# A decoder layer on one core: SBUF from the dynamic-transfer reserve, used for the last block's attention, ysT, five of FF1's joins and W1's pieces

## The chip, the core and the metric

The kernel runs on one core of one Trainium2 chip. The metric is device time in microseconds (us) of one execution, lower is better. Times before are the median of three runs; the profile is of one more execution. PE is TensorE, DVE is VectorE, ACT is ScalarE, POOL is GpSimd, SP is SyncE, which here issues nearly all transfers between HBM and SBUF.

## What is computed

One layer on x of 2048 rows by 1024 columns, in float32:

```python
a = rms_norm(h, pre_mix_g)
q, k, v, f, u_sg, v_sg = split(a @ w_in)
y_att = forgetting_attention(q, k, v, f + f_bias)        # 8 heads x 64, causal
y_sg = chunked_spatial_gating(u_sg, v_sg, ...)           # chunks of 128 rows
y = concat([rms_norm(y_att, att_out_g), rms_norm(y_sg, sg_out_g)])
h = h + rms_norm(y @ w_out, post_mix_g)
c = rms_norm(h, pre_ffn_g)
ff = square(relu(c @ w_ff1)) @ w_ff2                     # 1024 -> 4096 -> 1024
h = h + rms_norm(ff, post_ffn_g)
h = h + sigmoid(h @ ple_gate_w + ple_gate_b) * (p @ ple_w)
```

## The kernel before

**Precision.** Each large product is made of three matmuls (`mm3`, lines 102 to 106): operands are split into a higher half, a copy rounded to float32r, and a lower half, the rest. ACT mostly makes the higher halves and DVE the lower ones (`halves_of`, `evac_split`).

**Order.** The program is written in one order of emission, with fillers (`Filler`, `Spread`) that draw some steps of a side job per step of the main one. A planner then fixes each engine's list and the places of all tiles: it takes, for every engine, the earliest emitted instruction that its model of the time holds to be ready. So an instruction may stand far ahead of its place in the code, but on the chip each engine works through its list in order, and a wait holds up all that is behind it. SP's list of transfers is such a list too. A tile that is allotted where closed tiles were has to wait for the last use of those.

**Stages.** First the input projection, gating, and the maxima of the scores; then attention over four blocks of 512 rows, with the output projection of finished blocks (`project`, lines 695 to 810) drawn in between; then FF1, FF2 and the gate. FF1 and FF2 use a scheme with seven products in place of eight over 2x2 block matrices, so FF1's right operands B[m][k] (m = 1 to 7, k = 0 to 3) are sums and differences of pieces of the normed, turned h ("joins").

**Around the end of attention.** `finish(k)` (lines 676 to 693) takes a head's result, transposes it, divides it and stores it through `yo` to attS in HBM. `project(b)` goes over four tiles of 128 rows: it loads the attention rows `yn` (line 700), squares and norms them (706, 710), transposes them (766), splits them into `yaT` (769), and multiplies them and `ysT`, the gating's rows (714), with w_out, 16 steps of three matmuls for each tile, numbered `n`; the step at which the next tile is squared is `YSQ` (8), the one at which it is normed `YNO` (13). `ysT` has one place; its next load is emitted at its last use, step 11 of a tile. Results go through `z`, are normed and added to x, and are stored to hS (742 to 757). For the last block only the first row tile's last head goes into `yn` directly; the other three tiles come back from HBM.

With the last block's projection (`last_proj`, line 1122) runs `prep_first` (lines 1083 to 1095) as a filler, 16 parts over 54 steps: it loads pieces of hS into `px` tiles (three places) and `v_t`, `x_t`, scales them (POOL, 1013), transposes them (PE, 1018) and makes B for k = 0 and 1 on the spot (`join_now`), and stores the pieces of k = 2 and 3 to cS in HBM (1028). After the loop, `join_load` brings k = 2 back (1033), and `join(2)` starts with its three plain pieces. Then the pools of the projection and of w_out (`wide`) are closed. Only then are `w1p`, the three places of W1's split pieces, allotted (line 1134), as are the remaining B of k = 2 and 3 (`ctb`) and the joins' results j and inputs r (`jt`). The rest of join 2 and all of join 3 are emitted between the first seven products of FF1 (`join_rest`, `JR`).

FF1 (`run`, `left`, `ff1`) has 32 units; a unit has seven products of 4 x 3 matmuls. The first unit goes twice over its seven products, for k = 0, 1 first and k = 2, 3 after. `left` (1157 to 1181) makes W1's sums in `ws` on DVE (1170) and splits them into `w1p` (991 on ACT, 994 on DVE). The second half of the rows gets its B from `prep_next` (1097 to 1107), whose two held pieces lie in `px` too.

Of the kernel before, what the change touches and what calls it, by code (L numbers as in the profile page):

```python
# [9 lines left out]
F32 = mybir.dt.float32  # L10
# [24 lines left out]
def trunk(ctx, tc, x, p, w_in, f_bias, sg_ln_g, sg_ln_b, sg_w, sg_b, att_out_g, sg_out_g,  # L35
# [640 lines left out]
    def finish(k):  # L676

        b, h = heads[k]
        os = osp.tile([HD + 1, TB], F32, name="os")
        sc.copy(os, outs.pop(k)[:HD + 1])  # L680
        yield
        yt = pT.tile([P, 4, P], F32, name="pT")
        for tt in range(4):
            pe.transpose(yt[:, tt, :HD + 1], os[:, tt * P:(tt + 1) * P], ident[:HD + 1, :HD + 1])
        l = small.tile([P, 4], F32, name="l")
        ve.reciprocal(l, yt[:, :, HD])
        yo = small.tile([P, 4, HD], F32, name="yo")
        if k == len(heads) - 1:

            ve.tensor_tensor(tail_yn[0][:, AW - HD:], yt[:, 0, :HD], l[:, 0:1].broadcast_to([P, HD]), ALU.mult)  # L690
        ve.tensor_tensor(yo, yt[:, :, :HD], l.unsqueeze(2).broadcast_to([P, 4, HD]), ALU.mult)
        sy.dma_start(attS[b * TB:(b + 1) * TB, h * HD:(h + 1) * HD].rearrange("(a p) d -> p a d", p=P), yo)
        yield

    def project(b):

        def load(tt, width=AW):
            r0 = b * TB + tt * P
            yn = yp.tile([P, AW], F32, name="yn", bufs=2)
            sy.dma_start(yn[:, :width], attS[r0:r0 + P, :width])  # L700
            return yn
# [10 lines left out]
        def load_ys(tt):  # L712
            t = yp.tile([P, 4, 2, P], F32R, name="ysT")
            sy.dma_start(t.bitcast(F32), ysS[4 * b + tt])
            return t

        last = b == NB - 1
        ys_t = load_ys(0)
        yn = load(0, AW - HD if last else AW)
        if last:  # L720
            tail_yn.append(yn)
        yield
# [39 lines left out]
        for tt in range(4):  # L762
# [4 lines left out]
            if tt < 3:  # L767
                yn = load(tt + 1)
            ya_t = yp.tile([P, 2, 4, P], F32R, name="yaT", bufs=2)
# [10 lines left out]
            for hf, kcs in parts:  # L780
                if kcs[0] == 4:
                    nm = "pM" if pm_free and nb % 3 else "pW"
                    pss.append((pM if nm == "pM" else pW).tile([P, 512], F32, name=nm))
                    nb += 1
                for kc in kcs:
                    mm3(pss[hf], yT[kc], (w_o[kc][hf][:, 0], w_o[kc][hf][:, 1]), kc == 4, kc == 1)
                    if rest:
                        rest.popleft()()
                    if n in (6, 7):
                        xs.append(yp.tile([P, 512], F32, name="xt2", bufs=2))  # L790
                        sy.dma_start(xs[-1], x[r0:r0 + P, (n - 6) * 512:(n - 5) * 512])
                    if tt < 3:
                        if n == YSQ:
                            r_yn = square(yn)
                        if n == YNO:
                            normal(yn, r_yn)
                        if hf == 1 and kc == 7:
                            ys_t = load_ys(tt + 1)
                    if kc == 1:
                        zs[hf] = yp.tile([P, 512], F32, name="z2", bufs=2)  # L800
                        sc.copy(zs[hf], pss[hf])
                        junk = yp.tile([P, AW], F32, name="yjunk")
                        sc.activation(junk, zs[hf], AF.Square, accum_out=ss2[:, hf:hf + 1])
                    n += 1
                    yield
            tail(r0, zs, xs, ss2)
        while rest:
            rest.popleft()()
            if not last:
                yield  # L810

    YSQ, YNO = 8, 13
    MASKB = 4
    PREPT = 54
# [148 lines left out]
    ws = [fsm.tile([P, 4, P], F32, name=f"ws{e}") for e in range(2)]  # L963
    px = [w1q.tile([P, 4, P], F32, name=f"px{e}") for e in range(3)]

# [7 lines left out]

    _, w1raw = w1_places(w1q)

    LATE = (6, 3, 7, 2, 4)
    B = [[None] * KH for _ in range(8)]
    early = [ctx3.tile([P, 2, 512], F32R, name=f"B{m}_2") for m in (1, 3, 2)]  # L980
    kept = [ctx3.tile([P, 2, 512], F32R, name=f"B{m}_1") for m in LATE]
    for k in range(2):
        for m in range(1, 8):
            B[m][k] = kept[LATE.index(m)] if k and m in LATE else cta.tile([P, 2, 512], F32R, name=f"B{m}_{k}")
    for m, t in zip((1, 3, 2), early):
        B[m][2] = t
# [48 lines left out]
    def join(k, place, raws):  # L1035

        ra, rd, rc, rb = raws
        halves_of(B[1][k], ra, "pool", "dve")
        yield
        halves_of(B[3][k], rd, "act", "dve")  # L1040
        yield
        halves_of(B[2][k], rc, "act", "dve")
        yield
        t1, t2, t3, t4 = (place() for _ in range(4))
        for m, t, x, y, e in ((5, t1, rb, ra, po), (6, t2, rd, t1, ve), (7, t3, rd, rb, po), (4, t4, t2, rc, ve)):
            e.tensor_tensor(t, x, y, ALU.subtract)
            halves_of(B[m][k], t, "act", "dve")
            yield
# [31 lines left out]

    flat = [t.rearrange("p a b -> p (a b)") for t in px]

# [14 lines left out]
    def prep_next():  # L1097

        for k in (3, 2, 1, 0):
# [6 lines left out]

            yield from join_now(k, 1, place, done, flat[0], flat[1], px[2], px[2])

    raws, nraw, nleft = {}, 2, 0
    lefts = {}  # L1110
# [9 lines left out]
    load_w1(0, 0)  # L1120
    pfill = Filler(prep_first(), 16, PREPT)
    for n, _ in enumerate(last_proj):
        pfill.tick()
    pfill.drain()
    jraw = [flat[e] for e in range(3)] + [w1raw[1].rearrange("p k f -> p (k f)")[:, :512]]
    join_load(2, jraw)
    pl = []
    join2 = join(2, lambda: pl.pop(0), jraw)
    for _ in range(3):
        next(join2)  # L1130
    ph.close()
    pmph.close()
    mix_stack.close()
    w1p = w1_pieces(pool(w1s, "w1pp", side="right"))

# [104 lines left out]

    pl += [jt.tile([P, 512], F32, name=f"j{e}") for e in range(6)] * 2
    jraw3 = [jt.tile([P, 512], F32, name=f"r{e}") for e in range(4)]
    join_load(3, jraw3)

    def join_rest():
        join3 = join(3, lambda: pl.pop(0), jraw3)
        for _ in range(3):
            next(join3)
            yield
        for _ in range(4):  # L1250
            next(join2)
            yield
            next(join3)
            yield
# [103 lines left out]
    hold = first_of[NF + 2]  # L1358
    JR = (1, 1, 2, 2, 2, 2, 1)

    NEXT = [[(1, 2), (1, 3)], [(5, 2), (5, 3)], [(6, 1)], [(3, 1), (6, 2), (6, 3)], [(7, 1), (3, 2), (3, 3)],
            [(2, 1), (7, 2), (7, 3)], [(4, 1), (2, 2), (2, 3), (4, 2), (4, 3)]]
    for i, (u, n, ks) in enumerate(run):
        if i == len(JR):
# [3 lines left out]
            ctc = pool(fl, "ctc")  # L1368
            hqp = pool(fl, "hqp")
            for t in ((0, 0), (0, 1), (1, 0), (1, 1), 5, 6):  # L1370
                hq[t] = hqp.tile([P, 512], F32, name="hq" + str(t).strip("()").replace(", ", "_"))
# [50 lines left out]
    RR += [w1all.rearrange("p a k f -> p (a k f)")[:, e * 512:(e + 1) * 512] for e in range(4)]  # L1422
    wple = early + [kept[3]]
    wple = [wple[:2], wple[2:]]
# [197 lines left out]
```

## Time and profile before

| | |
|---|---|
| median of three runs | 2703.38 us (2702.57 to 2706.26) |
| profiled execution | 2701.87 us |
| its span | 2700.1 us |
| TensorE clock granted, mean | 0.989 |
| PE idle, 1123.7 to 1190.5 us (last block's projection) | 9.75 us of 66.80 |
| PE idle, 1190.5 to 1204.0 us (before FF1) | 13.5 us of 13.5 |
| DVE busy, 1190.5 to 1204.0 us | 13.06 us |

All times in the profile are microseconds from the start of the span. A row of the line of time has its start, its length, the engine, the line of the code (that of a helper, where one records the operation), the operation, out<-in, shapes and count; in brackets stands how long the engine was idle before it and what released it. A wait for several things is put down to the one that came last.

### The profile page before, as it was taken

The numbers are of one execution on the slowest core, as the hardware profiler recorded it, in microseconds if no ns is written. First come the engines' busy times: TensorE is split into PE (matmuls) and PEld (weight loads), VectorE is DVE, ScalarE is ACT, GpSimd is POOL, SyncE is SP. The second block draws the span as 40 slices with busy tenths as digits, with TensorE's granted clock in tenths as the row PEclk, the third lists the DMA queues.
The fourth block names the chain that finished last, engine by engine and source line by source line (L and its number), as shares of the span: only waits on it lengthen the run. The fifth ranks groups of instructions, "written<-read, shape, count | busy, mean of one in ns | idle before, by whom it ended". The sixth has DMA issues, their size and how long they took to land.

```text
span 2700.1 us, 37436 instructions
## 1 busy us (share of the span) xinstructions
PE 2613.7 (97%) x12316; PEld 2123.4 (79%) x12316; DVE 1841.5 (68%) x3212; ACT 1342.4 (50%) x2632; POOL 811.5 (30%) x695
## 2 busy tenths in 40 slices
PE   8999999999899999969999999999999999999999
PEld 7787978777677777757788788888888888888887
DVE  5547576866778655578888676668886596875443
ACT  6444433358777777555555554544445444453111
POOL 5444343510000000253444332325451171501211
PEclk9999999999999999989999999999999999999999
DMA  5565756598868766454665854447556654673331
GB/s 169 151 183 145 195 141 171 145 218 211 210 177 190 175 182 151 137 164 165 224 210 175 296 193 148 150 155 247 171 191 223 187 160 132 210 250 115 109 119 61
DMA packets 440611, 472.85 MB, mean 175 GB/s; under 512 B 155616, under 2 KB 269664, under 8 KB 440416
## 3 DMA queue, kind: packets, MB, share of 16 engines
q1 hardware_dynamic: 430179, 454.39, 57.0%
q10 hardware_dynamic: 10237, 16.07, 2.2%
q8 instruction: 97, 1.59, 0.3%
q14 instruction: 98, 0.80, 0.1%
HBM read 336.38 MB, written 133.96 MB: 174 GB/s over the span
## 4 chain that ended last, share of the span: by engine, by line
PE 53%; DMA 2%; DVE 1%; issue 1%; ACT 1%; POOL 0%; SPq 0%; DVEq 0%; ACTq 0%; POOLq 0%
PE pf L106 17%; PE pf L104 17%; PE pf L105 17%; PE pf L1470 1%; DMA w1raw<-in_w_ff_dram 0%; DMA px<-hS 0%; DMA cS<-px 0%; DVE w1p L994 0%; DMA B<-jS 0%; PE pf L1018 0%; DVE ws L1170 0%; DVE hq L1189 0%; DVE z L748 0%; POOL tmp L1068 0%; DMA ysT<-ysS 0%
## 5 line engine op out<-in xcount | busy, mean ns | idle before, releaser
L104 PE MATMUL pf<-B,w1p 128*128 128x512 f32 x752 | 298.3, 397 | 14.4 <-ACT w1p L991 13.6
L106 PE MATMUL pf<-B,w1p 128*128 128x512 f32 x752 | 296.1, 394 | 2.8 <-DVE w1p L994 2.7
L1197 POOL TENSOR_TENSOR hq<-hq,hq 128x512 f32<-128x512 f32 x128 | 197.0, 1550 | 335.4 <-ACT hq L1191 298.3
L105 PE MATMUL pf<-B,w1p 128*128 128x512 f32 x752 | 297.1, 395 | 0.0
L660 DVE TENSOR_TENSOR hl<-pr,hl 128x512 fp32r<-128x512 f32 (+1 forms) x320 | 191.9, 608 | 102.7 <-ACT hl L659 86.0
L100 POOL TENSOR_TENSOR wsp<-wraw,wsp 128x344 fp32r<-128x344 f32 (+1 forms) x176 | 200.1, 1154 | 192.0 <-ACT wsp L96 181.6
L651 ACT ACTIVATE pr<-pS,bias 128x512 f32<-128x512 f32 (+1 forms) x320 | 196.6, 623 | 106.1 <-PE pS L647 64.0
L172 DVE TENSOR_REDUCE mx<-pM 128x1 f32<-128x512 f32 (+3 forms) x288 | 169.8, 597 | 78.7 <-PE pM L169 78.0
L104 PEld LDWEIGHTS pf<-B,w1p 128*128 128x128 f32 x752 | 141.7, 188 | 48.9 <-ACT w1p L991 14.1
L104 PE MATMUL pacc<-wsp,wide 128*128 128x344 f32 (+1 forms) x480 | 166.7, 347 | 9.7 <-ACT ug L358 6.8
L104 PE MATMUL pf<-R,L 128*128 128x512 f32 x452 | 175.9, 389 | 0.0
L106 PE MATMUL pf<-R,L 128*128 128x512 f32 x452 | 175.8, 389 | 0.0
L105 PE MATMUL pf<-R,L 128*128 128x512 f32 x452 | 175.8, 389 | 0.0
L106 PEld LDWEIGHTS pf<-B,w1p 128*128 128x128 f32 x752 | 141.5, 188 | 37.5 <-DVE w1p L994 4.4
L105 PEld LDWEIGHTS pf<-B,w1p 128*128 128x128 f32 x752 | 141.7, 188 | 31.9
L106 PE MATMUL pacc<-wsp,wide 128*128 128x344 f32 (+1 forms) x480 | 162.7, 339 | 0.5 <-DVE wide L117 0.5
L105 PE MATMUL pacc<-wsp,wide 128*128 128x344 f32 (+1 forms) x480 | 162.4, 338 | 0.0
L659 ACT CAST hl<-pr 128x512 fp32r<-128x512 f32 (+3 forms) x272 | 146.6, 549 | 6.5 <-PE pO L674 0.8
L991 ACT CAST L<-lr 128x512 fp32r<-128x512 f32 x113 | 70.3, 622 | 149.6 <-PE pf L105 119.5
L994 DVE TENSOR_TENSOR L<-lr,L 128x512 fp32r<-128x512 f32 x113 | 96.1, 851 | 68.0 <-ACT L L991 67.7
L994 DVE TENSOR_TENSOR w1p<-ws,w1p 128x512 fp32r<-128x512 f32 (+1 forms) x136 | 117.4, 869 | 35.7 <-ACT w1p L991 33.8
L991 ACT CAST w1p<-w1raw 128x512 fp32r<-128x512 f32 (+1 forms) x123 | 73.4, 598 | 128.5 <-PE pf L105 124.2
(443 smaller groups left out, 7199.1 us busy)
## 6 DMA issues: line engine op xcount, KB each, us to landing
hidC<-hq SPq DMA_DIRECT2D x224, 256.0 KB
lr<-hidC SPq DMA_DIRECT2D x224, 256.0 KB
w1raw<-in_w_ff_dram SPq DMA_DIRECT2D x64, 512.0 KB
w1raw<-in_w_ff_dram SPq DMA_DIRECT2D x128, 256.0 KB
wraw<-in_w_in_dram SPq DMA_DIRECT2D x96, 256.0 KB
wraw<-in_w_in_dram SPq DMA_DIRECT2D x88, 172.0 KB
KM<-kS ACTq DMA_DIRECT2D x80, 132.0 KB
jS<-C SPq DMA_DIRECT2D x19, 512.0 KB
```

Of the source, the lines that this page charges most:

```text
L100: e.tensor_tensor(dst[:, 1], src, dst[:, 0].bitcast(F32), ALU.subtract)
L104: pe.matmul(ps, l[0], r[0], start=first, stop=False)
L105: pe.matmul(ps, l[0], r[1], start=False, stop=False)
L106: pe.matmul(ps, l[1], r[0], start=False, stop=last)
L172: ve.tensor_reduce(mx[:, tt, c:c + 1], ps[:, :full], AX.X, ALU.max)
L651: sc.activation(pr[:, off:], ps[:, off:], AF.Exp, bias=bias_of(b)[:, j, h:h + 1])
L659: sc.copy(hl[:, 0, off:], pr[:, off:])
L660: ve.tensor_tensor(hl[:, 1, off:], pr[:, off:], hl[:, 0, off:].bitcast(F32), ALU.subtract)
L991: sc.copy(dst[:, 0], src)
L994: (po if lo == "pool" else ve).tensor_tensor(dst[:, 1], src, dst[:, 0].bitcast(F32), ALU.subtract)
L1197: po.tensor_tensor(t, x, y, op)
L1470: pe.transpose(ps[:, kk], hts[t][g][:, kk * P:(kk + 1) * P], ident)
```

## The change

The kernel is built with 1 KB for each partition reserved for dynamic transfers in place of 16. In the places gained:

- The four `yn` tiles of the last block are loaded when its projection begins, without the last head's 64 columns; `finish` of the last head writes these into all four, and its store to attS goes. `yn` has four places, two before. For this block the next tile is squared at step 2 and normed at step 7.
- `ysT` has two places; a tile's `ysT` is loaded at the start of the tile before.
- Two of the three `px` tiles are the `ws` tiles; `prep_next` has two tiles of its own for its held pieces (`pxn`, in a pool that opens in FF1).
- `w1p` is allotted with `w1q`, before the projection's pools are closed.
- B[5][2] and B[6][2] lie in `ctx3` as B[1][2], B[3][2] and B[2][2] do. Join 2's loads and first five parts are emitted within the last projection's loop, once `prep_first` is used up; its subtractions take their place one at a time, the first two from the `tmp` pool. Two parts of join 2 and seven of join 3 stay in `join_rest`.

```diff
 def finish
+        if k == len(heads) - 1:
+            for tt in range(4):
+                ve.tensor_tensor(tail_yn[tt][:, AW - HD:], yt[:, tt, :HD], l[:, tt:tt + 1].broadcast_to([P, HD]), ALU.mult)
+            return
         yo = small.tile([P, 4, HD], F32, name="yo")
-        if k == len(heads) - 1:
-            ve.tensor_tensor(tail_yn[0][:, AW - HD:], yt[:, 0, :HD], l[:, 0:1].broadcast_to([P, HD]), ALU.mult)
         ve.tensor_tensor(yo, yt[:, :, :HD], l.unsqueeze(2).broadcast_to([P, 4, HD]), ALU.mult)
...
 def project
-            yn = yp.tile([P, AW], F32, name="yn", bufs=2)
+            yn = yp.tile([P, AW], F32, name="yn", bufs=4)
...
-            t = yp.tile([P, 4, 2, P], F32R, name="ysT")
+            t = yp.tile([P, 4, 2, P], F32R, name="ysT", bufs=2)
...
-        yn = load(0, AW - HD if last else AW)
         if last:
-            tail_yn.append(yn)
+            tail_yn.extend(load(tt, AW - HD) for tt in range(4))
+        yn = tail_yn[0] if last else load(0)
...
             if tt < 3:
-                yn = load(tt + 1)
+                yn = tail_yn[tt + 1] if last else load(tt + 1)
+                ys_next = load_ys(tt + 1)
...
-                        if n == YSQ:
+                        if n == (YSQL if last else YSQ):
                             r_yn = square(yn)
-                        if n == YNO:
+                        if n == (YNOL if last else YNO):
                             normal(yn, r_yn)
-                        if hf == 1 and kc == 7:
-                            ys_t = load_ys(tt + 1)
...
             tail(r0, zs, xs, ss2)
+            ys_t = ys_next
...
+    YSQL, YNOL = 2, 7
...
-    px = [w1q.tile([P, 4, P], F32, name=f"px{e}") for e in range(3)]
+    px = [*ws, w1q.tile([P, 4, P], F32, name="px")]
...
     _, w1raw = w1_places(w1q)
+    w1p = w1_pieces(w1q)
...
-    early = [ctx3.tile([P, 2, 512], F32R, name=f"B{m}_2") for m in (1, 3, 2)]
+    EARLY = (1, 3, 2, 5, 6)
+    early = [ctx3.tile([P, 2, 512], F32R, name=f"B{m}_2") for m in EARLY]
...
 def join
-        t1, t2, t3, t4 = (place() for _ in range(4))
-        for m, t, x, y, e in ((5, t1, rb, ra, po), (6, t2, rd, t1, ve), (7, t3, rd, rb, po), (4, t4, t2, rc, ve)):
+        ts = {}
+        for m, e in ((5, po), (6, ve), (7, po), (4, ve)):
+            t = ts[m] = place()
+            x, y = {5: (rb, ra), 6: (rd, ts[5]), 7: (rd, rb), 4: (ts.get(6), rc)}[m]
             e.tensor_tensor(t, x, y, ALU.subtract)
             halves_of(B[m][k], t, "act", "dve")
             yield
...
 def prep_next
-            yield from join_now(k, 1, place, done, flat[0], flat[1], px[2], px[2])
+            yield from join_now(k, 1, place, done, *pxn, px[2], px[2])
...
     pfill = Filler(prep_first(), 16, PREPT)
+    w1raw1 = w1raw[1].rearrange("p k f -> p (k f)")
+    jraw = [w1raw1[:, :512], w1raw1[:, 512:], v_t, px[2].rearrange("p a b -> p (a b)")]
+    pl = []
+    join2 = None
     for n, _ in enumerate(last_proj):
         pfill.tick()
-    pfill.drain()
-    jraw = [flat[e] for e in range(3)] + [w1raw[1].rearrange("p k f -> p (k f)")[:, :512]]
-    join_load(2, jraw)
-    pl = []
-    join2 = join(2, lambda: pl.pop(0), jraw)
-    for _ in range(3):
-        next(join2)
+        if not pfill.left and join2 is None:
+            pfill.drain()
+            join_load(2, jraw)
+            pl += [new_tmp() for _ in range(2)]
+            join2 = join(2, lambda: pl.pop(0), jraw)
+            jfill = Filler(join2, 5, 10)
+        elif join2 is not None:
+            jfill.tick()
+    while jfill.left:
+        jfill.tick()
...
-    w1p = w1_pieces(pool(w1s, "w1pp", side="right"))
...
-    pl += [jt.tile([P, 512], F32, name=f"j{e}") for e in range(6)] * 2
+    pl += [jt.tile([P, 512], F32, name=f"j{e}") for e in range(6)]
...
 def join_rest
-        for _ in range(4):
-            next(join2)
-            yield
+        for n in range(4):
+            if n < 2:
+                next(join2)
+                yield
             next(join3)
             yield
...
-    JR = (1, 1, 2, 2, 2, 2, 1)
+    JR = (1, 1, 2, 2, 1, 1, 1)
...
+            pxn = [hqp.tile([P, 512], F32, name=f"pxn{e}") for e in range(2)]
...
-    wple = early + [kept[3]]
+    wple = early[:3] + [kept[3]]
...
-    nc = _bacc.Bacc("TRN2", target_bir_lowering=False, num_devices=1)
+    nc = _bacc.Bacc("TRN2", target_bir_lowering=False, num_devices=1, dynamic_dma_scratch_size=1024)
```

More of the change, by code (lines that the diff above doesn't have):

```diff
@@ L984, in trunk @@
             B[m][k] = kept[LATE.index(m)] if k and m in LATE else cta.tile([P, 2, 512], F32R, name=f"B{m}_{k}")
-    for m, t in zip((1, 3, 2), early):
+    for m, t in zip(EARLY, early):
         B[m][2] = t
@@ L1079, in join_now @@
             yield
-    flat = [t.rearrange("p a b -> p (a b)") for t in px]
     def prep_first():
@@ L1105, in done @@
                     sy.dma_start(jS[m - 1, k - 1], place(m).bitcast(F32))
-            yield from join_now(k, 1, place, done, flat[0], flat[1], px[2], px[2])
+            yield from join_now(k, 1, place, done, *pxn, px[2], px[2])
+    pxn = None
     raws, nraw, nleft = {}, 2, 0
```

## Prediction

> **What bounds the kernel now.** I read the page first (span, engines), then the busy time by stage, then PE's line of time with its gaps, then what stands in the queues of ACT, DVE, POOL and SP ahead of each gap. The profiled execution took 2701.87 us, its span is 2700.1, and the median of three runs is 2703.38: the profile lies 1.5 us under the median, and I add that at the end.
>
> ```profile
> span 2700.1 us, 37436 instructions
> ...
> PE 2613.7 (97%) x12316; PEld 2123.4 (79%) x12316; DVE 1841.5 (68%) x3212; ACT 1342.4 (50%) x2632; POOL 811.5 (30%) x695
> ```
>
> PE is busy nearly throughout, so only its gaps and its slow clock can be won. By stage (columns: stretch, length, busy PE, PEld, DVE, ACT, POOL, granted clock, DMA share, GB/s):
>
> ```profile
> 1123.70:1190.50 66.80, 57.05 (x279) 45.78 (x277) 38.68 (x70) 32.90 (x73) 31.44 (x34) 0.95 0.70 214
> 1190.50:1204.00 13.50, 0.00 (x0) 0.00 (x0) 13.06 (x19) 7.67 (x18) 7.30 (x7) 0.61 0.50 165
> 1204.00:1212.00 8.00, 7.96 (x28) 6.42 (x29) 7.49 (x19) 3.77 (x10) 7.48 (x1) 0.80 0.00 0
> ...
> 1225.00:1600.00 375.00, 368.70 (x1609) 295.99 (x1608) 301.77 (x388) 194.54 (x339) 145.60 (x103) 1.00 0.63 216
> 1600.00:2450.00 850.00, 850.00 (x3723) 698.41 (x3722) 628.38 (x802) 397.45 (x710) 296.57 (x202) 1.00 0.57 183
> ```
>
> The last block's output projection (1123.7 to 1190.5) leaves PE idle for 66.80 - 57.05 = 9.75 us; between it and FF1 it does nothing for 13.5 us, in which DVE is busy for 13.06. From 1600 to 2450 there is nothing to win. PE's line of time names the gaps (start, length, engine, line, operation, [idle before <- releaser]):
>
> ```profile
> 1132.06 0.66 PE L1018 MATMUL pf<-ident,px 128*128 128x128 f32 x4 [1.52 <-POOL px L1013]
> ...
> 1158.60 0.66 PE L766 MATMUL pT<-ident,yn 128*128 128x128 f32 x4 [4.11 <-DVE yn L710]
> 1161.28 0.80 PE L104 MATMUL pW<-wide,ysT 128*128 128x512 f32 x1 [2.03 <-DMA ysT<-ysS]
> 1161.88 0.63 PE L105 MATMUL pW<-wide,ysT 128*128 128x512 f32 x1
> ...
> 1166.14 0.47 PE L106 MATMUL pW<-wide,ysT 128*128 128x512 f32 x1
> 1166.45 0.60 PE L1018 MATMUL pf<-ident,px 128*128 128x128 f32 x4
> 1166.88 0.60 PE L1018 MATMUL pf<-ident,x 128*128 128x128 f32 x4
> ...
> 1178.07 0.66 PE L766 MATMUL pT<-ident,yn 128*128 128x128 f32 x4 [0.72 <-DVE yn L710]
> 1179.13 0.50 PE L104 MATMUL pM<-wide,ysT 128*128 128x512 f32 x1 [0.40 <-DMA ysT<-ysS]
> 1179.47 0.39 PE L105 MATMUL pM<-wide,ysT 128*128 128x512 f32 x1
> 1179.70 0.39 PE L106 MATMUL pM<-wide,ysT 128*128 128x512 f32 x1
> ...
> 1190.02 0.39 PE L106 MATMUL pW<-wide,yaT 128*128 128x512 f32 x1
> 1204.04 0.79 PE L104 MATMUL pf<-B,w1p 128*128 128x512 f32 x1 [13.63 <-ACT w1p L991]
> 1204.63 0.63 PE L105 MATMUL pf<-B,w1p 128*128 128x512 f32 x1
> ...
> 1207.19 0.43 PE L105 MATMUL pf<-B,w1p 128*128 128x512 f32 x1
> ```
>
> Matmuls start 0.23 us apart at full speed (1179.47 to 1179.70). After the gaps of 4.11 and 2.03, 11 of them take from 1161.28 to 1166.14, 4.86 us where 11 x 0.23 = 2.5 would do: 2.3 lost to the clock. After the 13.63, 7 take from 1204.04 to 1207.19, 3.15 in place of 1.6: 1.5 lost.
>
> **Part 1: the last block's attention and ysT.** The four row tiles of the last block get places of their own: columns of the first seven heads are loaded at once, the last head is written into them by DVE, and its store, wait and three loads go. Their norm moves from steps 8 and 13 of a tile's 16 to 2 and 7. ysT gets a second place and its load goes to the tile's start. Now, SP, ACT and DVE read so:
>
> ```profile
> 1154.35 1.31 SPq L714 DMA_DIRECT2D ysT<-ysS  x1
> 1155.76 0.44 SPq L1012 DMA_DIRECT2D x<-hS  x1
> ```
>
> ```profile
> 1156.15 0.63 ACT L706 ACTIVATE yjunk<-yn 128x512 f32<-128x512 f32 x1
> ```
>
> ```profile
> 1157.79 0.75 DVE L710 SCALAR_TENSOR_TENSOR yn<-yn,ar,g_att 128x512 f32<-128x512 f32 x1 [0.73 <-POOL ar L111]
> ```
>
> The square that ends the 4.11 gap ran at 1156.15, after PE had already come to a halt at about 1154.5; six steps earlier is 6 x 3 x 0.23 = 4.1 us of PE's time, and the rows no longer have to be loaded for it, so the planner may put it earlier still. The ysT load was issued when its one place came free (1154.35) and PE waited to 1161.28; with two places it leaves one tile ahead. So 4.11, 2.03, 0.72, 0.40 and the 2.3 of slow clock go: 9.6 us. Added work is three 64-column products in DVE, each well under the 0.75 of the 512-column row, and one store less; I cost them at nothing, since the first tile is written first and PE has ysT products to do; without that cover, 1 us.
>
> What is late next: the fills of FF1's input, whose transposes (line 1018) stand in PE's order. The x tile was ready here:
>
> ```profile
> 1162.18 1.04 POOL L1013 TENSOR_TENSOR x<-x,hr_all 128x512 f32<-128x512 f32 x1 [3.16 <-DMA x<-hS]
> ```
>
> It was done at 1163.2, and PE took it at 1166.88. With 4.11 + 2.03 + 2.3 = 8.4 us gone ahead of it, PE wants it at 1158.4: 4.8 us too early, if nothing else moves. But its load left at 1155.76 behind the blocked ysT load (1.31) and SP's waits for the z rows, and SP now skips the attention round trip. Bounds 0 and 4.8; I take 2.5, the middle, for this and later such waits together. Two of the three px places become the ws tiles; their first load may leave earlier (0 to 1.5 of the 1.52 gap): I take 0. Part 1 gives 9.6 - 2.5 = 7.1.
>
> **Part 2: w1p allotted early.** Before, W1's pieces were placed where the projection's tiles (z, xt2, yjunk) had been, after these were closed. The queues show what that cost:
>
> ```profile
> 1200.05 0.63 ACT L751 ACTIVATE yjunk<-z 128x512 f32<-128x512 f32 x1 [3.11 <-DVE z L748]
> ...
> 1203.59 0.40 ACT L991 CAST w1p<-w1raw 128x256 fp32r<-128x256 f32 x1
> ```
>
> ```profile
> 1189.85 1.78 DVE L1046 TENSOR_TENSOR j<-px,j 128x512 f32<-128x512 f32 x1 [1.39 <-POOL j L1046]
> 1191.59 0.69 DVE L994 TENSOR_TENSOR B<-j,B 128x512 fp32r<-128x512 f32 x1
> ...
> 1195.09 3.42 DVE L745 SCALAR_TENSOR_TENSOR z<-z,zr,g_post 128x512 f32<-128x512 f32 x2 [0.44 <-POOL zr L742]
> ```
>
> The first cast of w1p stands behind the last tile's norm and the casts of the joins. With a place of its own, it needs only w1raw, loaded long before, and a free 0.40 us of ACT, then of DVE. ACT is busy for 32.90 of 66.80 in the projection, so there is room. I leave 0.8 (two such steps behind a busy engine) of the 13.63, and take the 1.5 of slow clock as gone: the 1.52 gap above shows no slow matmuls behind it. Bounds of the remaining gap: 0 and 5. Part 2 gives 12.8 + 1.5 = 14.3.
>
> **Part 3: five of k=2's seven joins moved ahead.** Their halves go to ctx3, out of the closed region, and the work runs in the projection's last tile; what remains is two of k=2 and seven of k=3. FF1's first unit runs k=0,1 first: 7 x 2 x 3 matmuls x 0.23 = 9.7 us, then k=2,3 product by product, 1.4 us each, so the last join must be there 9.7 + 6 x 1.4 = 18 us after the start. DVE did 13.06 + 7.49 = 20.6 us from 1190.5 to 1212, when the last joins were done. Taken away: the 1.78 subtraction and two lower halves of 0.69, 3.2 us, and three lower halves of w1p made ahead, 3 x 0.4 = 1.2. Added by the second pass: seven lower halves and four sums of 0.4, 4.4. So 20.6 us in 18: 3 us of waiting appear in the first unit (bounds 0, if DVE's gaps before the projection's end take them, and 6). POOL's and ACT's shares fit (7.30 and 7.67 of 13.5). SP's four loads for k=2 leave during the projection; those for k=3 still wait for the projection's weights to be used, as now. On ACT and DVE the moved joins stand behind late loads, and the last tile's norm and the first w1p behind them: that is in the bounds of part 2.
>
> The 1.78 beside POOL's subtraction, where such an operation else takes 0.69, is 1.1 us lost to the two running together. The Trainium skill, SBUF — State Buffer, section Who interferes with whom, says a DVE instruction with two SBUF inputs contends with a GpSimd one that reads SBUF, and the second to issue blocks; by that rule the moved subtraction costs the projection up to 1.1 us and the gain would be 1 less. I leave it out of the sum, since DVE is busy there for only 38.68 of 66.80.
>
> **Part 4: the 15 KB.** All transfers are of these queues (packets, MB, share of the 16 engines):
>
> ```profile
> q1 hardware_dynamic: 430179, 454.39, 57.0%
> q10 hardware_dynamic: 10237, 16.07, 2.2%
> q8 instruction: 97, 1.59, 0.3%
> q14 instruction: 98, 0.80, 0.1%
> ```
>
> None is POOL's, so I cost the smaller reserve at nothing; no row shows what it would cost otherwise. The Trainium skill, SBUF — State Buffer, section SBUF size: 192, 224, or 256?, calls these 16 KiB the descriptor ring of DMAs that GpSimd issues; no run here issues one.
>
> Later stages keep their work. The two pxn tiles replace px for the next half's joins, in places that open at the same step. PE's idle 375 - 368.7 = 6.3 us from 1225 to 1600 may shift by a few either way; taken at 0, bounds -3 and +3.
>
> **Sum.** -7.1 - 14.3 + 3 = -18.4: 2701.87 - 18.4 = 2683.5, and with 1.5 for the median 2685.0. From the bounds: all of 9.6, of 13.6 + 1.5 and of 1.5, with nothing given back, is -26.2 (2677); the worst of each, -(9.6 - 4.8) - (13.6 - 5) + 6 with the slow clock kept, is -7.4 (2696).
>
> **Rivals.**
> A, nothing given back (0.15): DVE is idle for 28 of 66.8 us in the projection, so it could take more ahead, and x may leave early. 2677.
> B, the input chain pins the projection (0.15): the waits for yn and ysT become waits for px, v and x (line 1018), 4.8 for x and as much again for the pair after it. For: x was done only 3.7 us before PE took it. Against: SP has fewer waits. Part 1 gives 0: 2685.0 + 7.1 = 2692.
> C, the start of FF1 stays late (0.08): the planner puts w1p behind the moved joins, whose loads land late, and the last norm. Now that norm's square (1200.05) comes 9.8 us after the projection's end (1190.02 and one step of 0.23); less the 3.2 of DVE moved away and with two steps of 0.4 the gap is 7.4. With 6 of waits in unit 0 and the slow clock kept: -7.1 - 6.2 + 6 = -7.3, or 2696. For: ACT and DVE do their lists in order. Against: ACT has room before the projection's end.
> D, no place is gained or everything waits as now (0.02): 2703.
> E, slower (0.04, with 0.01 for the unnamed): the order of the attention stage, where earlier blocks' projections run, is planned anew, since all blocks' ysT loads move and places shift. One wait there shows the price:
>
> ```profile
> 722.08 1.22 PE L169 MATMUL pM<-KM,QM 128*128 128x512 f32 x2 [4.84 <-DMA KM<-kS]
> ```
>
> ```profile
> PE pM L169 <- DMA KM<-kS: 5.8, 2, 4.8
> ```
>
> ```profile
> 720.00:740.00 20.00, 17.93 (x80) 13.69 (x81) 13.59 (x28) 9.85 (x20) 0.57 (x1) 0.85 0.69 189
> ```
>
> That is 4.84 and 20 x 0.15 = 3 of clock, 7.8 each. Three more of them are 23.4: 2685.0 + 23.4 = 2708. From the third on it turns the sign; against it, the list of PE's waits has two for this tile in the whole kernel, 5.8 us together.
>
> **How the numbers follow.** My forecast has 0.55, by itself 2680 to 2690. The range 2676 to 2697 takes in A, B and C and leaves out D, E and the tails. About 0.2% (5.4 us) is what a measurement of this kernel can tell from no change, so faster means under 2698.0: 0.55 + 0.15 + 0.15 and half of C, 0.89. Same: the other half of C and D, 0.06. Slower: 0.05.
>
> **What would show it.** Right: at line 766 no wait for yn over 1 us and none for ysT; the first pf<-B,w1p matmul within 2 us of the last yaT one, at full speed; k=2 halves (B) on DVE before that; the projection's end at about 1183. Wrong: line 1018 waiting for px, x or v over 4 us in sum (B); the first FF1 matmul behind a gap of 4 us or more, or second-pass matmuls waiting for B of k=3 over 5 us (C); attention's end later than now (E). The forecast is wrong if PE's idle time between 1123 and FF1's second unit shrinks by less than 12 or more than 24 us.

## The result, and the profile after

| | before | after |
|---|---|---|
| median | 2703.56 us (2699.94 to 2712.84, 11 executions) | 2691.93 us (2682.36 to 2698.43, 11 executions) |
| ratio, 95% interval | | 0.9943 (0.9929 to 0.9958) |
| profiled execution | 2701.87 us | 2682.36 us |
| its span | 2700.1 us | 2680.6 us |

The kernel became faster by 0.57%, with 0.42 to 0.71% in the interval: 11.6 us between the medians, 15.4 by the ratio. 2685.0 was forecast, 18.4 us of gain, with a range of 2676 to 2697. Two more series of the changed kernel, with the experiments, gave ratios of 0.9944 and 0.9945. The profiled execution of after is the lowest of its 11, 9.6 us under their median, so its span flatters the change. The differences must be read stage by stage and over several profiles.

The page of after has the same picture as before, PE busy nearly throughout:

```profile
span 2680.6 us, 37427 instructions
...
PE 2610.0 (97%) x12316; PEld 2123.4 (79%) x12316; DVE 1843.5 (69%) x3214; ACT 1341.6 (50%) x2632; POOL 806.6 (30%) x695
```

The first rows of PE's list of waits in after, from 1120 to 1340 (us in total, times, longest):

```profile
PE pf L1023 <- POOL x L1018: 4.9, 1, 4.9
PE pf L106 <- DVE w1p L999: 4.1, 3, 2.6
PE pf L104 <- ACT w1p L996: 3.9, 1, 3.9
PE pT L768 <- issue: 0.5, 1, 0.5
```

The waits for yn and ysT and the 13.63 us ahead of FF1 are gone; in their place stand one wait for x and waits for W1's pieces inside FF1. (Lines behind the new ones have moved: yn's transposes from 766 to 768, the fills' scaling and transposes from 1013 and 1018 to 1018 and 1023, the casts from 991 and 994 to 996 and 999, the joins from 1046 to 1053.) PE's line of time shows where:

```profile
1153.51 1.12 PE L1023 MATMUL pf<-ident,x 128*128 128x128 f32 x4 [4.92 <-POOL x L1018]
1154.28 0.78 PE L104 MATMUL pW<-wide,yaT 128*128 128x512 f32 x1
...
1177.61 0.39 PE L106 MATMUL pW<-wide,yaT 128*128 128x512 f32 x1
1177.84 0.39 PE L104 MATMUL pf<-B,w1p 128*128 128x512 f32 x1
...
1184.91 0.39 PE L105 MATMUL pf<-B,w1p 128*128 128x512 f32 x1
1189.20 0.50 PE L104 MATMUL pf<-B,w1p 128*128 128x512 f32 x1 [3.90 <-ACT w1p L996]
```

FF1 starts 0.23 us after the projection's last matmul, at full speed, and comes to a halt 7 us later. The stretches of after that answer to those of before (same columns):

```profile
1115.90:1177.90 62.00, 56.11 (x279) 46.41 (x278) 42.58 (x76) 35.50 (x78) 29.64 (x32) 0.94 0.62 195
1177.90:1189.50 11.60, 7.18 (x30) 5.16 (x29) 11.09 (x20) 6.37 (x16) 4.89 (x5) 1.00 0.49 159
1189.50:1200.00 10.50, 10.38 (x39) 7.92 (x38) 8.76 (x19) 4.25 (x11) 5.62 (x2) 0.84 0.18 53
```

DVE is busy for 11.09 of the 11.60 us after FF1's start, as it was for 13.06 of the 13.5 before it. What PE waits for behind the projection is still DVE's list; PE has now work of its own for part of that time.

**The stages.** From the first and last matmuls of each stage in each profile (us): the last block's projection, from the last matmul of attention to the last with yaT; the gap to the first of FF1; FF1's first half of the rows; and the sum of the three. The middle columns say which parts of the change a kernel has; "place" means that w1p doesn't lie on the projection's tiles.

| kernel | place | yn x4 | ysT x2 | joins | projection | gap | FF1, first half | sum |
|---|---|---|---|---|---|---|---|---|
| before | - | - | - | - | 66.4 | 14.0 | 323.1 | 403.5 |
| after | x | x | x | x | 61.8 | 0.2 | 329.6 | 391.6 |
| after, c0_again | x | x | x | x | 60.8 | 0.2 | 330.1 | 391.1 |
| after, c2_after_again | x | x | x | x | 62.6 | 0.2 | 327.6 | 390.4 |
| s1_reserve_only | x | - | - | - | 64.6 | 0.2 | 334.8 | 399.6 |
| s2_reserve_again | x | - | - | - | 64.0 | 0.3 | 331.4 | 395.7 |
| e1_no_rows | x | - | - | x | 63.5 | -11.9 | 337.9 | 389.5 |
| y1_one_ysT | x | x | - | x | 64.7 | -13.2 | 337.9 | 389.4 |
| y2_two_yn | x | - | x | x | 64.2 | 0.2 | 327.3 | 391.7 |
| e3_late_joins | x | x | x | - | 61.1 | 0.2 | 330.6 | 391.9 |
| e2_late_w1p | x | x | x | x | 62.1 | 0.2 | 331.5 | 393.8 |
| e4_w1p_on_rows | - | x | x | x | 60.6 | 10.3 | 326.4 | 397.3 |
| f1_two_pairs | x | x | x | x | 59.9 | 0.2 | 329.7 | 389.8 |
| n1_no_last_squares | x | x | x | x | 61.2 | 0.2 | 329.1 | 390.5 |

(Below zero: the planner drew FF1's first matmuls into the projection.) FF1's second half takes 317.6 to 322.2 in all, what follows it 853.5 to 853.7. What comes ahead of the projection is less steady: its end lay at 1123.6 in before and at 1115.8, 1124.3 and 1125.7 in the three profiles of after, with the same program. The three stages lost 11.9, 12.4 and 13.1 us: most of the gain is here. One profile each can't settle 3 us of the rest.

### The profile page after: what moved, and what is told of

Same layout as the page of the kernel before. It is cut to its first block, busy times and chain, and to the rows that moved or that the text cites. A ratio compares the mean times of both kernels' runs of the same rounds, so it can differ in the third digit from the quotient of the medians.

```text
span 2680.6 us, 37427 instructions
## 1 busy us (share of the span) xinstructions
PE 2610.0 (97%) x12316; PEld 2123.4 (79%) x12316; DVE 1843.5 (69%) x3214; ACT 1341.6 (50%) x2632; POOL 806.6 (30%) x695
## 4 chain that ended last, share of the span: by engine, by line
PE 53%; DVE 2%; DMA 1%; issue 0%; POOL 0%; ACT 0%; SPq 0%; DVEq 0%; ACTq 0%
PE pf L106 17%; PE pf L105 17%; PE pf L104 17%; DMA w1raw<-in_w_ff_dram 1%; PE pf L1485 1%; DVE w1p L999 0%; DMA B<-jS 0%; DVE ws L1183 0%; PE pf L1023 0%; DVE C L999 0%; DVE hq L1202 0%; PE pf L1478 0%; DVE z L750 0%; DVE v L1242 0%; DVE B L999 0%
```

## The experiments

Ratios are against the kernel before, run beside each; its medians were 2705.47 us (c0, e1 to e3), 2704.34 (s1, e4, f1, n1) and 2705.74 (y1, y2, s2, c2).

**The changed kernel again (c0_again).** No edit.

> The changed kernel once more, nothing edited. Its eleven runs spread from 2682.4 to 2698.4 us, and its first profile (span 2680.6) is the fastest of them. Theory: the spread is made of PE's waits for transfers between 560 and 1210 us (maxima, rows, FF1's input pieces), so this profile, if it is slower, is slower there and by those waits, and FF2 and after keep 853 us. Rival: the spread lies in FF1 or FF2, or in the clock; then the stages up to FF1's start take the same time as in the first profile within 2 us. Median expected 2690, plus or minus 4.

Measured: 2689.46 us (2686.70 to 2693.97), ratio 0.9944 (0.9929 to 0.9960). Its waits are those of after: 5.04 for x, 3.88 for w1p on ACT, 2.70 for w1p on DVE. They belong to the program. The spread between executions lies ahead of the projection, as the theory has it: attention ends 8.5 us later than in after (1124.3 against 1115.8) with the same list of PE, and PE is idle there for 52.2 us in place of 45.9, while the three stages and FF2 take as long. Which waits make the spread isn't shown.

**The 1 KB reserve alone (s1_reserve_only, s2_reserve_again).** The kernel before with

```diff
-    nc = _bacc.Bacc("TRN2", target_bir_lowering=False, num_devices=1)
+    nc = _bacc.Bacc("TRN2", target_bir_lowering=False, num_devices=1, dynamic_dma_scratch_size=1024)
```

> The kernel before with one argument changed: 1 KB in place of 16 reserved. Nothing else is edited, but the places move apart, so that W1's split pieces no longer lie on the projection's tiles, and ACT's list now has their first two casts before the last block's projection. Theory: it was that overlap that made the gap of 13.6 us before FF1; it goes here too (under 1 us), with the waits for yn and ysT still there, and the kernel is 8 to 13 us faster than before, within 4 of the whole change. Rival: yn, ysT and the moved joins make the gain, then the gap stays at 9 or more and the time is within 4 us of before.

> The kernel before with a reserve of 1 KB and nothing else, a second time, on the chip of the changed kernel. If the four combinations (neither, rows and ysT alone, joins alone, both) are read rightly from the two calls before, this one lies 10 to 12 us above the changed kernel run beside it and 3 to 5 under the kernel before. If its first reading (2700.24, 12 executions that lie 20 us apart) was an accident of the chip, it lies within 5 of the changed kernel's: then the places and the joins ahead would be worth little, and the reserve would be the change.

Measured: 2700.24 us, ratio 0.9986 (0.9974 to 0.9998), and 2702.56, ratio 0.9987 (0.9975 to 0.9999); the second is 11.6 above the changed kernel and 3.2 under the kernel before on the same chip, so the first reading was no accident. The gap is gone (0.2 and 0.3 us) by this line alone, with w1p allotted where it was before in the code: with 15 KB more, its place no longer falls on the projection's tiles. Yet the kernel gains only 0.14%. The waits of PE in s2 from 1120 to 1340 and PE's line of time say where it went:

```profile
PE pT L766 <- DVE yn L710: 4.0, 2, 3.2
PE pf L106 <- DVE w1p L994: 3.8, 3, 3.1
...
PE pf L106 <- DVE zr L741: 1.8, 1, 1.8
```

```profile
1188.35 0.39 PE L106 MATMUL pW<-wide,yaT 128*128 128x512 f32 x1
1188.57 0.39 PE L104 MATMUL pf<-B,w1p 128*128 128x512 f32 x1
...
1195.09 0.50 PE L106 MATMUL pf<-B,w1p 128*128 128x512 f32 x1 [1.80 <-DVE zr L741]
...
1196.12 0.63 PE L104 MATMUL pf<-B,w1p 128*128 128x512 f32 x1
...
1199.11 0.59 PE L105 MATMUL pf<-B,w1p 128*128 128x512 f32 x1
1199.54 0.40 PE L106 MATMUL pf<-B,w1p 128*128 128x512 f32 x1
...
1203.22 0.80 PE L106 MATMUL pf<-B,w1p 128*128 128x512 f32 x1 [3.06 <-DVE w1p L994]
```

FF1 begins 13.7 us sooner after the projection and then stops twice for DVE, with slow matmuls behind each stop: its first half grows from 323.1 to 334.8 and 331.4. A gap of 13.7 us was closed and 8.3 to 11.7 came back behind it.

**The place, and the moment (e4_w1p_on_rows, e2_late_w1p).** e2 allots w1p after the projection, as before, in the changed kernel; e4 does so too, with an unused tile of 8 KB ahead that pushes it onto the projection's tiles:

```diff
-    w1p = w1_pieces(w1q)
...
     mix_stack.close()
+    w1x0 = pool(w1s, "w1x0", side="right")               # e4 alone
+    spare = w1x0.tile([P, 4, 512], F32, name="spare")    # e4 alone
+    w1p = w1_pieces(pool(w1s, "w1pp", side="right"))
```

> Part 2 undone: W1's split pieces are allotted after the projection's pools are closed, as before; all else as changed. Theory: PE's gap between the projection and FF1 comes back with 9 to 13 us, in exchange the waits inside FF1's first unit (3.9 and some) shrink by about 4; 6 to 10 us slower than the changed kernel. Rival: it was the joins on ACT and DVE that made the gap, so with five of them moved ahead the gap stays under 4 and the loss under 3.

> The changed kernel, with W1's split pieces allotted after the projection's pools are closed and pushed 8 KB further by an unused tile, so that they lie on the projection's last tiles again; all else, the moved rows and joins too, as changed. In e2_late_w1p only the moment of allotting was undone, the place was the same. Theory: the gap before FF1 comes back with 8 to 13 us and FF1's first unit gets 3 to 5 shorter: 5 to 9 us slower than the changed kernel. Rival: with five joins out of the way the first casts come soon after the projection, gap under 4, loss under 3.

Measured: e2 2689.61 us, ratio 0.9947 (0.9930 to 0.9965), as the changed kernel, with a gap of 0.2. So its rival has the numbers, but not the cause: e4 has the joins moved as well. e4 measured 2697.97, ratio 0.9974 (0.9964 to 0.9985), 0.3% above the changed kernel. The first rows of e4's list of PE's waits from 1120 to 1340 are

```profile
PE pf L104 <- ACT w1p L995: 10.0, 1, 10.0
PE pf L1022 <- POOL x L1017: 4.7, 1, 4.7
```

The gap is back at 10.3, and the moment of allotting does nothing. That the place was the cause of the gap is shown from both sides: by s1, where many places move, and by e4, whose edit moves w1p alone.

**Part 1 undone, and its halves (e1_no_rows, y1_one_ysT, y2_two_yn).** y1 has one place for ysT and the load at the end of a tile; y2 has two places for yn, the way through HBM, and the old steps; e1 has both:

```diff
-            t = yp.tile([P, 4, 2, P], F32R, name="ysT", bufs=2)      # y1, e1
+            t = yp.tile([P, 4, 2, P], F32R, name="ysT")
...
-            yn = yp.tile([P, AW], F32, name="yn", bufs=4)            # y2, e1
+            yn = yp.tile([P, AW], F32, name="yn", bufs=2)
```

> Part 1 undone: two yn places, the last three row tiles stored and loaded again, one ysT place, squares and norms at the old steps; all else as changed. Theory: the last block's projection goes back from 62.0 to about 66 us, with waits of PE for yn (about 4) and ysT (about 2), and the kernel is 4 to 8 us slower than the changed one. Rival: FF1's input pieces (px, v, x) pin the projection anyhow, so it stays at 62 plus or minus 1.5 and the time is the same as the changed kernel's. The attention stage ended 8 us earlier in the changed kernel's profile; if that comes of ysT's and yn's places in the earlier blocks, it goes back too, and the loss is 12 or more.

> The changed kernel with ysT back at one place and its load back at the end of a tile; the four places for the last block's rows stay, and so do the 1 KB reserve and the joins ahead. Theory 1 (ysT's second place is what took the wait for KM near 722 to 730 out of the attention stage): that wait is back at 3.9 to 4.8 us, TensorE's clock from 670 to 760 is 0.94 to 0.96 in place of 0.97 to 0.98, and the time is 4 to 6 us above the changed kernel's run beside it. Theory 2 (the four rows for yn did it, by fewer loads on SP's queue): no wait for KM over 1 us, and the time lies within 2 us of the changed kernel's. Both: one wait for ysT of about 2 us is back in the last projection, and the wait for x there is shorter by about as much.

> The changed kernel with the last block's rows back at two places, through DRAM, and their norm back at steps 8 and 13; ysT keeps its two places and early load. Theory 1: no wait for KM over 1 us near 722 to 730, and a time within 2 us of the changed kernel's, since in the last projection the wait for yn of about 3 us takes the place of the wait for x of 4.9. Theory 2: the wait for KM is back at 3.9 to 4.8 us and the time is 4 to 6 us above.

Measured: e1 2694.99 us, ratio 0.9959 (0.9944 to 0.9975); y1 2693.69, 0.9958 (0.9941 to 0.9974); y2 2691.80, 0.9947 (0.9931 to 0.9963); c2_after_again beside the last two 2691.00, 0.9945 (0.9930 to 0.9960). e1 is 5.5 us above c0, as expected, but the intervals overlap, and its projection takes 63.5 and not 66. In the three stages they take 389.4 to 391.7, as long as the changed kernel (390.4 to 391.6): without yn's places, PE waits 3.65 us for yn (y2) and not for x. Without ysT's, it waits 3.42 and 1.95 for ysT and not for x. With the other parts in place, the four places of yn are worth nothing that can be measured. What ysT's second place is worth, if anything, lies elsewhere; the wait for KM early in attention goes with it. Before's row is in the prediction; here are those of e1 and of y1:

```profile
727.61 1.22 PE L169 MATMUL pM<-KM,QM 128*128 128x512 f32 x2 [3.87 <-DMA KM<-kS]
```

```profile
725.45 0.73 PE L169 MATMUL pM<-KM,QM 128*128 128x512 f32 x2 [2.12 <-DMA KM<-kS]
```

With one place for ysT this wait, at 721 to 730 us, was 4.84, 3.87, 4.28, 3.13 and 2.12 us (five profiles), with two at most 1.8 (nine). Later waits for KM, at 855 to 893 us, stay with two places too: 1.5 to 2.5 us in c0, 2.91 in n1. ACT's list, which issues KM's loads, shows how, before and then y2:

```profile
713.29 0.29 ACTq L165 DMA_DIRECT2D KM<-kS  x1
717.34 0.29 ACTq L165 DMA_DIRECT2D KM<-kS  x1
```

```profile
708.83 0.29 ACTq L165 DMA_DIRECT2D KM<-kS  x1
718.14 0.29 ACTq L165 DMA_DIRECT2D KM<-kS  x1
```

With two places the loads leave some 10 us apart and PE doesn't come to a halt; in after PE has ysT products to do between the maxima there. So theory 1 holds for the wait, and theory 2 is out (y2: 0.44 us). But y1's wait is 2.12 and not 3.9 to 4.8, the clock from 670 to 760 us is 0.98 in both, where theory 1 had 0.94 to 0.96 for y1, and y1 is 2.7 us above c2 and not 4 to 6, with intervals that overlap: the wait is shown, its worth isn't.

**The joins back behind the projection (e3_late_joins).** Part 3 undone, the rest kept:

```diff
-    EARLY = (1, 3, 2, 5, 6)
+    EARLY = (1, 3, 2)
...
+    pfill.drain()
+    join_load(2, jraw)
+    join2 = join(2, lambda: pl.pop(0), jraw)
+    for _ in range(3):
+        next(join2)
```

> Part 3 undone: join 2 is emitted after the projection's loop again, three of its parts before and four within FF1's first products, its subtractions in the old places; all else as changed. Theory: FF1 starts at once (gap under 2), but its first unit waits 3 to 5 us more for B of k=2 and 3 on DVE, and the kernel is 2 to 5 us slower than the changed one. Rival: the joins take the place of w1p on ACT and DVE, so the gap before FF1 comes back with 6 or more.

Measured: 2695.88 us (2691.69 to 2699.44, 9 executions), ratio 0.9963 (0.9951 to 0.9975), 6.4 above the median of c0, measured beside it; the intervals of the ratios overlap by a little. But its three stages take 391.9, as in after, and up to attention's end its PE list is that of after. In its one profile most of the extra lies ahead of the projection, where the program is the same. So the joins' worth on top of the rest stays open, between nothing and some 6 us. On the bare reserve they seem to be worth more: e1, which adds them (and the new places of px and w1p), has 389.5 where s1 and s2 have 399.6 and 395.7, with a ratio of 0.9959 (to 0.9975) against 0.9986 (from 0.9974). The rows and ysT alone (e3) bring that sum to 391.9 as well. By these profiles, one of each kernel, either part takes the waits out of these stages that the other would, and both together take no more.

**The wait for x taken away (f1_two_pairs).** The second round of fills gets input places of its own, so that x's load needn't wait for its place:

```diff
-    v4, x4 = (t.rearrange("p (a b) -> p a b", b=P) for t in (v_t, x_t))
+    hx = [[t.rearrange("p (a b) -> p a b", b=P) for t in ts] for ts in ((v_t, x_t), (pb[:, :512], pb[:, 512:]))]
...
-    jraw = [w1raw1[:, :512], w1raw1[:, 512:], v_t, px[2].rearrange("p a b -> p (a b)")]
+    jraw = [x_t, v_t, w1raw1[:, :512], px[2].rearrange("p a b -> p (a b)")]
```

> The changed kernel with a second pair of places for the input pieces of prep_first's second round (the halves of the idle w1raw tile), so that the load of x no longer waits for the first round's transposes and stands no longer behind them; join 2's inputs swap places with them. Theory: PE's wait of 4.9 us for x (line 1023) in the last block's projection and the slow clock behind it go, the projection takes 55 to 57 in place of 61 to 62 us, and the kernel is 4 to 7 us faster than the changed one. Rival: the next piece in the chain (ws, v) makes PE wait instead, and the projection stays above 59.

Measured: 2691.35 us (2688.71 to 2693.22), ratio 0.9954 (0.9941 to 0.9967). No gain that can be measured; the projection takes 59.9, 1.8 us under the mean of after's three. The wait went, and another came (a row of PE's list of waits, then ACT's line of time ahead of it):

```profile
PE pM L104 <- ACT yaT L116: 3.3, 1, 3.3
```

```profile
1173.54 0.62 ACT L996 CAST B<-tmp 128x512 fp32r<-128x512 f32 x1 [2.36 <-DVE tmp L1073]
1174.95 1.14 ACT L996 CAST B<-tmp 128x512 fp32r<-128x512 f32 x2 [0.79 <-POOL tmp L1075]
1176.00 0.61 ACT L996 CAST B<-w1raw 128x512 fp32r<-128x512 f32 x1
...
1176.99 0.60 ACT L116 ACTIVATE yaT<-pT 128x512 fp32r<-128x512 f32 x1
```

yaT's higher half stands on ACT behind the casts of the fills, and those wait for DVE and POOL. So the theory (55 to 57 us) failed, and of the rival the bound of 59 held, with another wait than the one it named: when the load is no longer late, the lists of DVE, ACT and POOL are the next limit, 1.8 us behind.

**The last tile's squares left out (n1_no_last_squares).** In after ACT's square of the last tile's z stands ahead of the cast of w1p for which PE waits 3.90. For the last tile alone:

```diff
+                if r0 == S - P:
+                    ve.memset(hss[:, hf:hf + 1], 512.0)
+                    return
```

> The changed kernel without the squares of the last row tile's two halves of h on ACT (their sums are set to a constant, so the last 128 rows are scaled by a constant before FF1). Theory: these two stand in ACT's list ahead of a cast of w1p and wait there for DVE's last norm; without them the wait of 3.9 us in FF1's first pass goes, and from FF1's start to the first matmul of the second half it takes 326 us in place of 330, 3 to 5 us less in all. Rival: DVE is the bound there, so the same wait comes back as one for DVE's halves of w1p, and less than 1.5 us is won.

Measured: 2691.21 us (2687.86 to 2696.38), ratio 0.9957 (0.9944 to 0.9970). The cast came early, and PE waited at nearly the same place (the 31st matmul of FF1, the 29th in after) for DVE's half of the piece before, which stands behind the same norm:

```profile
1198.44 0.79 PE L106 MATMUL pf<-B,w1p 128*128 128x512 f32 x1 [4.49 <-DVE w1p L1002]
```

So ACT was only the name that came last in the list of waits. DVE's list is the limit, as the rival has it.

**The changed kernel beside the last four (c2_after_again).** No edit.

> The changed kernel as it is, on the same chip as the other three: 2689 to 2692, 12 to 15 us under the kernel before. Its one profile shows the wait for x of 4.8 to 5.2 us in the last projection, no idle time of TensorE before FF1, and a wait of 3.9 for ACT's cast of w1p in FF1's first 20 us, as in its two profiles before; were one of these absent, it would be no property of the program.

Measured as told above; its waits are 5.46 for x and 3.90 for w1p on ACT. One thing is its own: a wait for KM of 1.80 at 729 us, which c0 and after don't have there.

## Why the prediction was right, and which terms were off

By the means of after's three profiles, in the prediction's terms: the projection 4.7 us shorter (7.1 forecast), the gap 13.8 (12.8), and FF1's first half 6.0 longer, where 1.5 shorter for the clock and 3 longer for waits, 1.5 longer in all, was forecast. That is 12.5 in place of 18.4: 2.4 of the miss lie in part 1 and 4.5 in FF1's start, and the gap gave 1.0 more than forecast.

**The signs and the number.** The signs for right came: no wait for yn over 1 us and none for ysT, and FF1 starts 0.23 us behind the projection at full speed. The first sign for wrong came as well, a wait for x of over 4 us. PE's idle time from attention's last matmul to FF1's second unit fell from 23.3 us to 10.4, 10.8 and 11.2, so by 12.1 to 12.9, just inside the 12 to 24 that were allowed. The median lies 1.9 us above the 2680 to 2690 that the forecast named for itself and on the 2692 of rival B. That it meets B's number is luck: B puts the whole loss into the projection, and most of it came in FF1's start.

**Part 2, the gap: right**, cause and size. It was one line of the change that did it, the reserve; the new place in the code did nothing (e2), since with 1 KB the old one gives the same place.

**Part 1: the removed waits right, the give-back too small.** At line 768 no wait for yn and none for ysT is left, as forecast. The step that was mis-sized is "Bounds 0 and 4.8; I take 2.5, the middle": the wait for x came at 4.92, 5.04 and 5.46, beyond its upper bound, with slow matmuls behind it, where the prediction had counted the 2.3 of slow clock as gone for good. The load of x left right behind the stores of z, the loads of xt and that of ysT, and landed 6.5 us after it was issued (SP's list, then POOL's):

```profile
1142.98 0.94 SPq L751 DMA_DIRECT2D hS<-z  x2
...
1145.49 0.38 SPq L716 DMA_DIRECT2D ysT<-ysS  x1
1145.92 0.50 SPq L1017 DMA_DIRECT2D x<-hS  x1
```

```profile
1152.42 1.04 POOL L1018 TENSOR_TENSOR x<-x,hr_all 128x512 f32<-128x512 f32 x1 [3.21 <-DMA x<-hS]
```

This is half of rival B, which foresaw 4.8 for x and as much again for the pair after it: the first came, the second didn't. And f1 shows that the wait isn't worth its length: without it the projection is 1.8 us shorter and the kernel not measurably faster.

**Part 3 and FF1's start: the wrong work was counted.** "So 20.6 us in 18: 3 us of waiting appear in the first unit" takes the last join as what FF1 needs last. The waits came, but earlier, and for W1's later pieces. Part 2 costed the first piece of w1p alone; the next ones stand behind the last tile's norm in DVE's and ACT's lists:

```profile
1183.59 2.78 DVE L747 SCALAR_TENSOR_TENSOR z<-z,zr,g_post 128x512 f32<-128x512 f32 x2 [0.45 <-DMA w1raw<-in_w_ff_dram]
1186.29 2.35 DVE L750 TENSOR_TENSOR z<-z,xt 128x512 f32<-128x512 f32 x2
...
1189.77 0.41 DVE L999 TENSOR_TENSOR w1p<-ws,w1p 128x256 fp32r<-128x256 f32 x1
```

```profile
1183.62 0.61 ACT L996 CAST B<-r 128x512 fp32r<-128x512 f32 x1
1188.13 0.63 ACT L753 ACTIVATE yjunk<-z 128x512 f32<-128x512 f32 x1 [3.90 <-DVE z L750]
...
1188.76 0.39 ACT L996 CAST w1p<-w1raw 128x256 fp32r<-128x256 f32 x1
```

```profile
1184.11 3.38 POOL L1053 TENSOR_TENSOR j<-r,r 128x512 f32<-128x512 f32 x2
1191.00 4.61 POOL L759 TENSOR_TENSOR hr_all<-hr_all,mhalf 128x1 f32<-128x1 f32 x1 [3.51 <-DVE hr_all L758]
```

ACT's idle 3.90 us and PE's have one source: both wait for z. DVE's four instructions on z take 5.13 us, beside two of POOL's joins. A pair at line 747 took 1.40 us at 1140.11, and a single one at line 750 takes 0.69, so 2.8 would do for the four. In e4 POOL's joins begin later, at 1193.32, and there the four take 3.04:

```profile
1190.88 1.76 DVE L747 SCALAR_TENSOR_TENSOR z<-z,zr,g_post 128x512 f32<-128x512 f32 x2 [0.73 <-POOL zr L744]
1192.56 1.28 DVE L750 TENSOR_TENSOR z<-z,xt 128x512 f32<-128x512 f32 x2
```

So 2.1 to 2.35 us of the norm go to DVE and POOL running together. That PE's 3.90 us would shrink by as much is worked out from rows and not shown: in e4 FF1 starts too late to tell, and there three lower halves of r (line 998), beside the joins in the norm's place, took 4.02 us where one alone takes 0.69. The Trainium skill, SBUF — State Buffer, section Who interferes with whom, has it that a DVE instruction with two inputs in SBUF contends with a GpSimd one that reads SBUF, and that the ports they share are an exclusive lock. The rows come close to that: two joins of POOL at 1.31 (one beside an idle DVE, at 1188.51 in before) and DVE's 2.8 are 5.4 us one after another, and together they ran from 1183.59 to 1188.64, 5.05. The prediction weighed this rule for the projection and left it out of the sum since DVE had room there; the cost came where DVE had none.

**Part 4 and the later stages: right.** s1 and s2 are not slower than before, and what follows FF1 takes the same 853.5 to 853.7 us with 1 KB as with 16.

**The rivals.** A, nothing given back, is refuted by the waits for x and w1p. C's gap did not come, but its waits in FF1's first unit did. D is out. E foresaw a price in attention of 7.8 us for each new wait for KM; the order there did change, the other way: the one wait of 4.84 went, and the later one of 0.96 became 1.31 to 2.46 in the three profiles of after.

## What to carry to other kernels

A gap ahead of a stage says what its first instruction waits for, not what the stage is short of: here 13.6 us went with one line, and 8 to 12 came back in the half of FF1 behind it, most of them within 40 us, since the engine that fed the stage had been busy throughout the gap (DVE, 13.06 of 13.5 us). Before a gap is booked as won, the feeding engine's list has to be laid against the next instructions' needs, piece by piece, and not only the first and the last. And when two edits each remove a different wait on the same chain, measure each alone and both: here either gave nearly all that the two together gave in these stages.

## What the runs showed of the hardware

**The price of a wait in clock.** Between 1115 and 1355 us of the 14 profiles, all 27 waits of PE of 3.0 us or more were followed by matmuls at about half speed, all ten from 1.4 to 1.76 by none, and of 13 from 1.80 to 2.70 six were and seven not (two more lie in another's slow stretch). The same wait of 2.61 us at the same place of the list had a slow stretch in e2, beginning a microsecond later, and none in after. First e2, then after:

```profile
1331.34 0.50 PE L106 MATMUL pf<-B,w1p 128*128 128x512 f32 x1 [2.61 <-DVE w1p L998]
...
1332.38 0.57 PE L104 MATMUL pf<-B,w1p 128*128 128x512 f32 x1
1332.74 0.63 PE L105 MATMUL pf<-B,w1p 128*128 128x512 f32 x1
...
1336.02 0.40 PE L104 MATMUL pf<-B,w1p 128*128 128x512 f32 x1
```

```profile
1327.95 0.50 PE L106 MATMUL pf<-B,w1p 128*128 128x512 f32 x1 [2.61 <-DVE w1p L999]
...
1330.14 0.39 PE L106 MATMUL pf<-B,w1p 128*128 128x512 f32 x1
```

In e2 the stretch lasts from 1332.38 to 1336.0, 3.6 us, in which matmuls start 0.43 us apart in place of 0.23: 1.7 us lost. The Trainium skill, TensorE: Matmul & The Clock Gate, Part 1, tells of a free-running window of some 3.4 us, with half speed after an idle one and full speed after a busy one. A window that doesn't start with the wait fits the chance of it, and the stretch of 3.6 fits its length. That a wait of 1.80 us, as s2's, is enough doesn't fit a window that has to be idle from end to end; here the measurement stands.

**A tiny POOL instruction held up for 4 us.** POOL's power of one column (line 759) took 4.61 us at 1191.00 in after, beside DVE's unbroken list of two-input instructions; the same line took 0.55 at 1162.48. It was 4.61 in c0 and c2 as well, and 8.31 in before. But in e4 it took 0.93 beside DVE's two-input instructions, so these alone don't make it. No wait of PE is put down to it here.
